# A two-layer encoder trunk on one core: stores issued later, the bias masked in DRAM, and softmax sums applied after the value product

## The chip, the cores and the metric

The kernel runs on one core of a Trainium2 chip as one program. The metric is the device time of a run in microseconds, taken as the median of several runs. A separate, profiled execution of the same program gives the views that are quoted here; its clock starts at its first instruction.

## The reference

The input is x, 2048 rows of 1024 float32. Layer A is a gated MLP that mixes rows within groups of 128; layer B is a chunked attention whose K and V come once from the residual stream after layer A. The change touches layer B and the projections around it. Reduced to what matters (16 heads of 64, chunks of 64 rows, a band of 9 chunks):

```python
h = rms_norm(x, b_norm_g)
q, z = split(h @ w_qz)                      # 1024 each
bias = rel_bias[:, clip(rel, -256, 256) + 256]
...
sc = q * 64 ** -0.5 @ kc.T + bias           # kc, vc: this chunk and the 8 before it
sc = where(valid, sc, -1e30)
o = softmax(sc) @ vc
x = x + (o * silu(z)) @ w_out
out = rms_norm(x, final_norm_g)
```

## The kernel before

Every product runs on TensorE (PE) as three matmuls of split operands: high x high, low x high, high x low (`mm3`, lines L113 to L115). The high half is a rounding copy on ScalarE (ACT), the low half a subtraction on VectorE (DVE). The 2048 rows are four tiles t = 0 to 3 of 512 rows. The order in each engine's queue is written by the framework's scheduler from the order of the program and its own estimates; at run time each engine takes its queue strictly in order, and all DMAs are issued by SyncE (SP) from one such queue. A store whose data is not ready therefore keeps every later load waiting.

The stages follow one another in the profile:

- Layer A until about 1340 us. Beside it, `rel` is copied 16 times into DRAM as `reld` (128 equal rows of 768 per head).
- The V projection (`vp`), 1340 to 1550 us: four tiles by Strassen's seven products. `v_left` splits sums of x into `Shv` and `Slv`, `v_evict` builds `v` and stores it to `vhd` (L1156). Beside it `norm` and `block` prepare the next tile of x and store it to `xtd`, and `o_sums` prepares sums of the output weight and stores their halves to `ows` (L306).
- Attention of tile 0, 1550 to about 1760 us, and of tiles 1 to 3, to about 2617 us. Tiles 1 to 3 each carry the output projection of the tile before (`bo`).
- The tail, to 2709.6 us: the output projection of tile 3.

An attention tile has eight pairs p of heads, and a pair has eight steps u (two heads, four blocks of 128 rows). `take` interleaves matmuls of the next pair's projections (`project`: Q and K, `gate`: Z) with the steps. In tile 0 the weights are loaded raw (`weights`, L210), scaled in place on GpSimd (POOL, `scaled`, L184), stored to `wk` for the later tiles (L212) and split into `wh_b` on ACT (L199) and `wl_b` on DVE (L200); four raw buffers serve these loads and others. In tiles 1 to 3 the scaled weights are loaded (L208).

Step u issues `score(u + 2)`: the product Q K into PSUM `s` (one buffer); DVE adds the bias, negates and takes the row minimum (L1328); ACT takes the exponential and its row sum `sl` (L1335); DVE inverts it (L1338); POOL scales the row of probabilities with it (L1339). The bias tile of a head is loaded as a skewed view of `reld` (`load_bias`, L1297) and two corners of 64x64 are overwritten on POOL (L1301, L1302). Then `flip(u)` transposes the block on PE (L1355, PSUM `tp`, one buffer), ACT copies it rounded (L1358), DVE subtracts (L1359). `value` multiplies with V after four steps (L1379); two adds join the halves (L1388, L1389); after the second head the gate multiplies 0.5 Z (L1396) and `og` is stored to `ogd` (L1401). For the last two pairs of tile 3 `last_og` takes the place of that store. Finished rows are normalized in `finish` (y loaded from `x2d` at L1519, scaled at L1522, stored to `out` at L1526).

## Time and profile before

| | us |
|---|---|
| median of 3 runs | 2712.83 (2712.39 to 2716.46) |
| the profiled execution | 2711.34 |
| its span, first to last instruction | 2709.6 |
| PE busy in the span | 2624.9 |
| mean granted clock of TensorE | 0.988 |

Times in the views are from the start of the span. Engines are PE, PEld (its weight load, which overlaps), DVE, ACT, POOL and SP; SPq is SP's own queue. In a row of the timeline the brackets hold the idle time of the engine before the instruction and what ended it. In a group's row, after the count, stand the busy time, the mean in ns, and the idle time before with its releasers. In the waits, after the colon, stand the total in us, the number of times and the longest. In the DMA rows stand the count, the size of one and the median time from issue to landing. The last figure but two of a row of stretches is the granted clock, then the DMA share and GB/s.

### The profile page before, as it was taken

The numbers are of one execution on the slowest core, as the hardware profiler recorded it, in microseconds if no ns is written. First come the engines' busy times: TensorE is split into PE (matmuls) and PEld (weight loads), VectorE is DVE, ScalarE is ACT, GpSimd is POOL, SyncE is SP. The second block draws the span as 40 slices with busy tenths as digits, with TensorE's granted clock in tenths as the row PEclk, the third lists the DMA queues.
The fourth block names the chain that finished last, engine by engine and source line by source line (L and its number), as shares of the span: only waits on it lengthen the run. The fifth ranks groups of instructions, "written<-read, shape, count | busy, mean of one in ns | idle before, by whom it ended". The sixth has DMA issues, their size and how long they took to land. (4 is left out here: it accounts for less than half of the span.)

```text
span 2709.6 us, 38048 instructions
## 1 busy us (share of the span) xinstructions
PE 2624.9 (97%) x12960; PEld 2194.7 (81%) x12960; DVE 1882.2 (69%) x2937; ACT 1295.4 (48%) x2296; POOL 890.3 (33%) x874
## 2 busy tenths in 40 slices
PE   8999999999999999999989989999999999999997
PEld 7788888888888888888867777788888888788875
DVE  5655676676677668667677867676678667866676
ACT  5422243433524435333355466556556555655553
POOL 3512335143351414114044344323233224223243
PEclk9999999999999999999999999999999999999999
DMA  8898999989988879768677788776688667766577
GB/s 300 310 333 328 347 363 326 329 310 351 326 310 287 304 261 324 284 214 288 238 250 259 253 270 280 254 229 200 224 265 271 200 216 241 254 199 203 180 233 244
DMA packets 274769, 735.51 MB, mean 271 GB/s; under 512 B 29584, under 2 KB 61328, under 8 KB 274576
## 3 DMA queue, kind: packets, MB, share of 16 engines
q1 hardware_dynamic: 274576, 733.09, 78.0%
q8 instruction: 103, 1.69, 0.2%
q14 instruction: 90, 0.74, 0.1%
HBM read 540.56 MB, written 181.93 MB: 267 GB/s over the span
## 5 line engine op out<-in xcount | busy, mean ns | idle before, releaser
L113 PE MATMUL P<-T,S 128*128 128x512 f32 x1248 | 495.0, 397 | 2.1 <-ACT S L376 2.1
L115 PE MATMUL P<-T,S 128*128 128x512 f32 x1248 | 489.4, 392 | 0.0
L114 PE MATMUL P<-T,S 128*128 128x512 f32 x1248 | 488.2, 391 | 0.6 <-DVE T L379 0.6
L1339 POOL TENSOR_SCALAR pr<-pr,sl 128x640 f32<-128x640 f32 (+4 forms) x256 | 198.4, 775 | 576.8 <-DVE sl L1338 498.8
L113 PE MATMUL pj<-hh_b,wh_b 128*128 128x512 f32 x768 | 321.4, 418 | 3.2 <-ACT wh_b L199 2.4
L115 PE MATMUL pj<-hh_b,wl_b 128*128 128x512 f32 x768 | 306.2, 399 | 0.1
L114 PE MATMUL pj<-hl_b,wh_b 128*128 128x512 f32 x768 | 305.2, 397 | 0.0
L1335 ACT ACTIVATE pr<-pr,nm 128x640 f32<-128x640 f32 (+4 forms) x256 | 195.4, 763 | 179.2 <-DVE nm L1328 174.3
L115 PEld LDWEIGHTS P<-T,S 128*128 128x128 f32 x1248 | 234.8, 188 | 50.3
L113 PEld LDWEIGHTS P<-T,S 128*128 128x128 f32 x1248 | 235.2, 188 | 46.7 <-ACT S L376 2.3
L114 PEld LDWEIGHTS P<-T,S 128*128 128x128 f32 x1248 | 235.1, 188 | 46.5 <-DVE T L379 1.0
L1359 DVE TENSOR_TENSOR pt<-tp,pt 128x640 fp32r<-128x640 f32 (+4 forms) x256 | 188.9, 738 | 63.4 <-ACT pt L1358 60.0
L1328 DVE CUSTOM_DVE_ANT_0 pr<-s,bias 128x640 f32<-128x640 f32 (+4 forms) x256 | 188.1, 735 | 31.9 <-PE s L1320 26.1
L1358 ACT CAST pt<-tp 128x640 fp32r<-128x640 f32 (+4 forms) x256 | 159.1, 621 | 64.7 <-PE tp L1355 60.9
L1355 PE MATMUL tp<-ident,pr 128*128 128x128 f32 x1120 | 167.1, 275 | 19.8 <-DVE pt L1359 12.5
L1355 PEld LDWEIGHTS tp<-ident,pr 128*128 128x128 f32 x1120 | 131.2, 141 | 53.3 <-issue 17.7
L115 PEld LDWEIGHTS pj<-hh_b,wl_b 128*128 128x128 f32 x768 | 146.2, 190 | 32.9 <-DVE wl_b L200 0.5
L1379 PEld LDWEIGHTS pv<-pt,V 128*128 128x128 f32 x896 | 145.2, 191 | 24.6 <-ACT pt L1358 6.1
L113 PEld LDWEIGHTS pj<-hh_b,wh_b 128*128 128x128 f32 x768 | 146.8, 191 | 21.7 <-ACT wh_b L199 3.5
L1379 PE MATMUL pv<-pt,V 128*128 128x256 f32 (+3 forms) x896 | 156.1, 323 | 5.6 <-ACT pt L1358 3.7
L114 PEld LDWEIGHTS pj<-hl_b,wh_b 128*128 128x128 f32 x768 | 146.9, 191 | 17.3
L200 DVE TENSOR_TENSOR wl_b<-raw_b,wh_b 128x1024 fp32r<-128x1024 f32 x96 | 126.8, 1320 | 33.9 <-ACT wh_b L199 32.8
(284 smaller groups left out, 5719.2 us busy)
## 6 DMA issues: line engine op xcount, KB each, us to landing
S<-hsd SPq DMA_DIRECT2D x288, 512.0 KB, 5.1
rw<-in_w_a SPq DMA_DIRECT2D x108, 512.0 KB, 6.3
A<-ytd SPq DMA_DIRECT2D x72, 512.0 KB, 5.8
raw_b<-wk SPq DMA_DIRECT2D x72, 512.0 KB, 4.0
hsd<-S SPq DMA_DIRECT2D x56, 512.0 KB, 4.2
V<-vhd SPq DMA_DIRECT2D x56, 512.0 KB, 5.3
wh_bo<-ows SPq DMA_DIRECT2D x50, 512.0 KB, 4.0
wl_bo<-ows SPq DMA_DIRECT2D x50, 512.0 KB, 5.5
```

Of the source, the lines that this page charges most:

```text
L113: first = mm(ps, lh, rh, start=first, stop=False)
L114: mm(ps, lh, rl, start=False, stop=False)
L115: mm(ps, ll, rh, start=False, stop=last)
L200: tv(wl[:], raw[:], wh[:].bitcast(F32), op=sub)
L1328: nc.vector.tensor_tensor_reduce(out=pr[:, c0:].rearrange("p (a b) -> p a b", a=nseg), in0=ps[:, :nseg, :w], in1=bias[:, c0:].rearrange("p ...
L1335: nc.scalar.activation(pr[:, c0:], pr[:, c0:], AF.Exp, scale=-1.0, bias=nm[:], accum_out=sl[:])
L1339: nc.gpsimd.tensor_scalar(pr[:, c0:], pr[:, c0:], sl[:], 1.0, op0=ALU.mult, op1=ALU.mult)
L1355: tpose(tp[:, b, :], pr[:, b * P : (b + 1) * P], ident[:])
L1358: nc.scalar.copy(oh, tp[:, b0:5, :].rearrange("p a b -> p (a b)"))
L1359: nc.vector.tensor_tensor(pt[:, 2560 + o + b0 * P : 2560 + o + 640], tp[:, b0:5, :].rearrange("p a b -> p (a b)"), oh.bitcast(F32), op=ALU ...
L1379: mm(po[:, q0 * P : q1 * P], vtl[t, p][:, i, hs], rhs, start=(i == blocks[0] and j == 0), stop=(i == 7 and j == 1),)
```

## The change

- **Bias.** The host now lays out the skewed bias, 128 x 640 per head. During layer A it is copied to `biasd[h]`, and two DMAs of 64x64 write the mask into each copy from a small table `negd`. A tile's bias is one plain load of 320 KB; the 128 memsets are gone, and the load is issued one step later (qb 2 instead of 1).
- **Probabilities.** They stay unnormalized. The row sums of a pair's eight steps go to the eight columns of one tile `sums`, inverted together at u = 7 (32 reciprocals of 128x8 in place of 256 of 128x1). `flip` at u = 6 (5 for the last pair) transposes the sums as well, ACT copies the 8x128 result to `rc`, one DMA stores it to `rcd`, and two DMAs read it back, broadcast over 64 partitions each, as `w` (128x512). The sums are complete by then, because `score` runs two steps ahead of `flip`.
- **Gate.** `gated` runs at u = 1 of the next pair: POOL multiplies w by Z, DVE multiplies 0.5 og32 by that.
- **Held stores.** `hold(n, ...)` puts a store in a list, `tick()` counts projection steps, and after n of them the store is issued with an ordering dependency (no wait at run time) on the last matmul written. Held are the stores to `xtd` (tiles above 0), `wk`, `ows`, `owf`, `vhd`, `khd`, `ogd`, `x2d`, `out` (tiles below the last), the copies of Q between partitions, and the trip of the sums. `release_all()` issues what is left before a load of y and at the ends of stages.

Counted in the compiled programs, PE gets 32 more instructions, ACT 32 more, SP 129 more DMAs; DVE 224 fewer and POOL 351 fewer.

```diff
-    reld = [dram.tile([P * 768], F32, name=f"reld{h}") for h in range(NH)]
+    rcd = [dram.tile([NPAIR, 8 * P], F32, name=f"rcd{t}") for t in range(NT)]
+    biasd = [dram.tile([P, 640], F32, name=f"biasd{h}") for h in range(NH)]
+    negd = dram.tile([P, 64], F32, name="negd")
...
-    mm, tpose = nc.tensor.matmul, nc.tensor.transpose
+    tpose = nc.tensor.transpose
+    pe = [None]
+    def mm(*args, **kw):
+        ins = nc.tensor.matmul(*args, **kw)
+        pe[0] = ins.ins.name
+        return ins
...
+    held = []
+    def tick():
+        for x_ in held:
+            x_[0] -= 1
+        for x_ in [x_ for x_ in held if x_[0] <= 0]:
+            release(x_)
+    def release(x_):
+        held.remove(x_)
+        for args in x_[1]:
+            ins = nc.sync.dma_start(*args)
+            tc.add_manual_dep(
+                ins.ins, pe[0],
+                mybir.DependencyInfo(mybir.DependencyClass.NoSync, mybir.DependencyReason.DATA),
+                reason="order",
+            )
+    def hold(n, *todo):
+        held.append([n, todo])
+    def release_all():
+        while held:
+            release(held[0])
...
             nc.scalar.copy(x3[:, ks, :], half[h][:])
-        nc.sync.dma_start(xtd[t][b][:], xt[:])
+        if t:
+            hold(4, (xtd[t][b][:], xt[:]))
+        else:
+            nc.sync.dma_start(xtd[t][b][:], xt[:])
...
             paced_by_pj(scaled(raw, (bg if c else kg)[:, :, :]))
-            nc.sync.dma_start(wk3[p][c][:], raw[:])
+            hold(1, (wk3[p][c][:], raw[:]))
         hi = split_in(raw, *w)
...
             if ph == 5:
-                nc.sync.dma_start(owf[q][:, cs], src)
+                hold(3, (owf[q][:, cs], src))
             hi, lo = (s_place(f"so{u}_{ph}{x_}") for x_ in "hl")
...
             for n, y_ in enumerate((hi, lo)):
-                nc.sync.dma_start(ows[ph, q][:, n, cs], y_[:].bitcast(F32))
+                hold(3, (ows[ph, q][:, n, cs], y_[:].bitcast(F32)))
...
+        def mask():
+            ng = acc_tile("ng")
+            nc.gpsimd.memset(ng[:, 0:64], NEG)
+            nc.sync.dma_start(negd[:], ng[:, 0:64])
+        at(start[3, 1] + 2, mask)
         at(start[1, 6] + 8, uz_open)
...
                 start[3 + h // 6, 1] + 3 + 9 * (h % 6),
-                lambda h=h: nc.sync.dma_start(
-                    reld[h].rearrange("(p c) -> p c", c=768), rel[h, :].partition_broadcast(P)
-                ),
+                lambda h=h: nc.sync.dma_start(biasd[h][:], rel[h]),
+            )
+            at(
+                start[3 + h // 6, 1] + 8 + 9 * (h % 6),
+                lambda h=h: [
+                    nc.sync.dma_start(biasd[h][0:64, 576:640], negd[0:64, :]),
+                    nc.sync.dma_start(biasd[h][64:128, 0:64], negd[64:128, :]),
+                ],
             )
...
                     )
-                nc.sync.dma_start(
-                    vhd[t][:, 4 * c : 4 * c + 4, 2 * jp + r, :], v[:].bitcast(F32)
-                )
+                hold(3, (vhd[t][:, 4 * c : 4 * c + 4, 2 * jp + r, :], v[:].bitcast(F32)))
...
             ):
+                tick()
                 if t + 1 < NT and i in (1, 4, 7, 10):
...
                     todo.pop(0)()
+        release_all()
         pt4x.close()
...
                 )
-                for x_ in (qh, ql):
-                    nc.sync.dma_start(x_[r2, :].bitcast(F32), x_[r, :].bitcast(F32))
+                hold(2, *((x_[r2, :].bitcast(F32), x_[r, :].bitcast(F32)) for x_ in (qh, ql)))
                 qt[t, p, hd] = (qh, ql)
...
                 if t + 1 < NT:
-                    nc.sync.dma_start(khd[t][p][hd], kx[:, T:].bitcast(F32))
+                    hold(4, (khd[t][p][hd], kx[:, T:].bitcast(F32)))
                 if t > 0:
...
         prs = {}
+        sums = {}
         pts = {}
...
                 bias[:],
-                reld[h][127 : 127 + P * 767].rearrange("(p c) -> p c", c=767)[:, :640],
+                biasd[h][:],
             )
-            nc.gpsimd.memset(bias[0:64, 576:640], NEG)
-            nc.gpsimd.memset(bias[64:128, 0:64], NEG)
             bias_t[t, h] = bias
...
             h = 2 * p + hd
-            if qb == 1 and (h + 1 < NH or t + 1 < NT):
+            if qb == 2 and (h + 1 < NH or t + 1 < NT):
                 load_bias(t + (h + 1) // NH, (h + 1) % NH)
...
             nm = sm.tile([P, 1], F32, tag="nm", name=f"nm{t}_{h}_{qb}", bufs=4)
-            sl = sm.tile([P, 1], F32, tag="sl", name=f"sl{t}_{h}_{qb}", bufs=4)
+            if u == 0:
+                sums[t, p] = sm.tile([P, 8], F32, tag="sl", name=f"sl{t}_{p}", bufs=2)
             nc.vector.tensor_tensor_reduce(
...
             nc.scalar.activation(
-                pr[:, c0:], pr[:, c0:], AF.Exp, scale=-1.0, bias=nm[:], accum_out=sl[:]
+                pr[:, c0:], pr[:, c0:], AF.Exp, scale=-1.0, bias=nm[:],
+                accum_out=sums[t, p][:, u : u + 1],
             )
-            nc.vector.reciprocal(sl[:], sl[:])
-            nc.gpsimd.tensor_scalar(
-                pr[:, c0:], pr[:, c0:], sl[:], 1.0, op0=ALU.mult, op1=ALU.mult
-            )
+            if u == 7:
+                nc.vector.reciprocal(sums[t, p][:], sums[t, p][:])
             prs[t, h, qb] = pr
...
                 tpose(tp[:, b, :], pr[:, b * P : (b + 1) * P], ident[:])
+            if u == sums_at(t, p):
+                tpose(tp[0:8, 5, :], sums[t, p][:], ident[:])
             o = qb * 640
...
             )
+            if u == sums_at(t, p):
+                inverse(t, p, tp[0:8, 5, :])
+        def sums_at(t, p):
+            return 5 if t + 1 == NT and p + 1 == NPAIR else 6
+        def inverse(t, p, src):
+            rc = sm.tile([8, P], F32, tag="rc", name=f"rc{t}_{p}", bufs=1)
+            nc.scalar.copy(rc[:], src)
+            w = zt[t, p, 1] = sb.tile([P, T], F32, tag="og", name=f"w{t}_{p}", bufs=2)
+            trip = [(rcd[t][p].rearrange("(a b) -> a b", b=P), rc[:])] + [
+                (
+                    w[hd * 64 : hd * 64 + 64, :],
+                    rcd[t][p, hd * T : hd * T + T].partition_broadcast(64),
+                )
+                for hd in range(2)
+            ]
+            if t + 1 == NT and p + 1 == NPAIR:
+                for args in trip:
+                    nc.sync.dma_start(*args)
+            else:
+                hold(1, trip[0])
+                hold(6, *trip[1:])
...
             nc.vector.tensor_tensor(og32[r, :], po[r, :], ot[r, :], op=ALU.add)
-            if hd == 0:
-                return
-            if hd == 1 and t + 1 == NT and p >= 6:
-                last_og(p, og32, zt[t, p])
-            elif hd == 1:
-                og = sb.tile([P, T], F32, tag="og", name=f"og{t}_{p}", bufs=2)
+        def gated(t, p):
+            og32, og = og32s[t, p], zt[t, p, 1]
+            tg(og[:], og[:], zt[t, p][:], op=ALU.mult)
+            if t + 1 == NT and p >= 6:
+                last_og(p, og32, og)
+            else:
                 nc.vector.scalar_tensor_tensor(
-                    og[:], og32[:], 0.5, zt[t, p][:], op0=ALU.mult, op1=ALU.mult
+                    og[:], og32[:], 0.5, og[:], op0=ALU.mult, op1=ALU.mult
                 )
                 o4 = og[:].rearrange("p (j r s) -> p r j s", j=2, r=2)
-                for r_ in range(2):
-                    nc.sync.dma_start(ogd[t][:, r_, p], o4[:, r_])
+                hold(3, *((ogd[t][:, r_, p], o4[:, r_]) for r_ in range(2)))
...
                 if not last:
-                    nc.sync.dma_start(x2d[t][b][:, c * 512 : c * 512 + 512], y)
+                    hold(2, (x2d[t][b][:, c * 512 : c * 512 + 512], y))
                 if (r, c) in ((1, 0), (0, 1)):
...
                 else:
+                    release_all()
                     y = sb.tile([P, 2, 512], F32, tag="bx", name=f"y{t}_{b}", bufs=1)
...
                     r0 = t * T + b * P
-                    nc.sync.dma_start(out[r0 : r0 + P, cs], y[:, c, :])
+                    if last:
+                        nc.sync.dma_start(out[r0 : r0 + P, cs], y[:, c, :])
+                    else:
+                        hold(2, (out[r0 : r0 + P, cs], y[:, c, :]))
...
                     return
+                tick()
...
             for _ in gen:
-                pass
+                tick()
...
                     done = max(done, upto)
+                    if u == 1 and before:
+                        gated(*before)
                     if u == 4:
...
         value(*before, 1)
+        gated(*before)
         run(gen)
...
         run(outs[NT - 1])
+        release_all()
...
     lo = 639 - 256
-    relr = relr[:, np.clip(np.arange(768) - lo, 0, relr.shape[1] - 1)]
+    cols = np.arange(640)[None, :] - np.arange(P)[:, None] + 127
+    relr = relr[:, np.clip(cols - lo, 0, relr.shape[1] - 1)]
     arrays = {
```

## The prediction

> **What bounds the kernel now.** I read the page's busy times first, then a table of stretches, then the waits, and last the timeline at the places where PE stood still.
>
> ```profile
> PE 2624.9 (97%) x12960; PEld 2194.7 (81%) x12960; DVE 1882.2 (69%) x2937; ACT 1295.4 (48%) x2296; POOL 890.3 (33%) x874
> ```
>
> PE is busy for 97% of the span. A change that leaves PE's matmuls alone can only win idle time and time at a low granted clock, so I look for both by stage. The columns are the stretch, its length, the busy time of PE, PEld, DVE, ACT and POOL, the granted clock, the DMA share and GB/s:
>
> ```profile
> 100.00:1340.00 1240.00, 1236.72 (x5809) 1028.77 (x5808) 840.03 (x1058) 461.64 (x731) 366.94 (x251) 1.00 0.86 310
> 1340.00:1550.00 210.00, 187.67 (x840) 151.75 (x839) 155.12 (x224) 110.93 (x218) 84.74 (x63) 0.96 0.71 246
> 1550.00:1600.00 50.00, 44.70 (x217) 35.83 (x216) 32.64 (x71) 27.80 (x59) 22.30 (x28) 1.00 0.87 277
> 1600.00:1650.00 50.00, 45.18 (x213) 36.54 (x212) 33.28 (x80) 29.00 (x63) 20.83 (x29) 0.93 0.80 267
> 1650.00:1700.00 50.00, 46.10 (x226) 37.39 (x225) 38.41 (x91) 31.57 (x74) 24.35 (x33) 0.94 0.87 289
> 1700.00:1760.00 60.00, 55.80 (x274) 44.10 (x272) 39.90 (x93) 35.97 (x75) 20.85 (x30) 0.98 0.75 248
> 1760.00:2617.00 857.00, 847.43 (x4627) 729.77 (x4627) 619.52 (x1139) 504.71 (x912) 258.00 (x346) 0.99 0.69 223
> 2617.00:2709.60 92.60, 70.36 (x321) 54.91 (x319) 64.56 (x105) 39.55 (x77) 40.83 (x38) 0.93 0.74 253
> ```
>
> Layer A has 3.3 us of idle PE in 1240 us: what the change puts there (mask and bias copies) lies under it. The idle time is in the V projection (22.3 us), attention tile 0 (5.3 + 4.8 + 3.9 + 4.2 = 18.2 us), tiles 1 to 3 (9.6 us in 857) and the tail (22.2 us). The clock takes more: 7% and 6% of 50 us in tile 0, 6.5 us, and 7% of 92.6 us in the tail, 6.5 us.
>
> What holds PE in tile 0 (start, duration, engine, line, what ended the idle time before):
>
> ```profile
> 1558.33 0.14 POOL L1301 MEMSET bias<- 64x64 f32 x1 [21.24 <-DMA bias<-reld]
> 1560.68 1.05 ACT L199 CAST wh_b<-raw_b 128x1024 fp32r<-128x1024 f32 x1 [3.43 <-POOL raw_b L184]
> 1564.70 0.39 PE L1320 MATMUL s<-K,Qh 128*128 128x256 f32 x1 [2.21 <-DVE nm L1328]
> 1593.74 1.96 DVE L200 TENSOR_TENSOR wl_b<-raw_b,wh_b 128x1024 fp32r<-128x1024 f32 x1 [0.20 <-ACT wh_b L199]
> 1596.90 0.41 PE L1355 MATMUL tp<-ident,pr 128*128 128x128 f32 x2 [2.08 <-POOL wo L315]
> 1640.95 1.90 POOL L184 TENSOR_TENSOR raw_b<-raw_b,bg 128x1024 f32<-128x1024 f32 x1 [0.60 <-DMA raw_b<-in_w_kqz]
> 1643.97 1.23 DVE L200 TENSOR_TENSOR wl_b<-raw_b,wh_b 128x1024 fp32r<-128x1024 f32 x1 [2.75 <-ACT wh_b L199]
> 1645.87 0.74 PE L1355 MATMUL tp<-ident,pr 128*128 128x128 f32 x4 [1.99 <-POOL pr L1339]
> 1692.64 1.90 POOL L184 TENSOR_TENSOR raw_b<-raw_b,bg 128x1024 f32<-128x1024 f32 x1 [3.50 <-DVE sl L1338]
> 1695.67 0.80 PE L113 MATMUL pj<-hh_b,wh_b 128*128 128x512 f32 x1 [1.65 <-ACT wh_b L199]
> ```
>
> POOL runs in order. At 1558 a mask memset that waits for its bias holds up the weight scaling (raw_b) behind it, and so ACT's wh_b and everything after; at 1596 and 1645 the transposes wait for a probability scale queued behind other POOL work; at 1692 raw_b stood behind a scale that waited for its sum. Four times PE pays: 2.21 + 2.08 + 1.99 + 1.65 = 7.9 us.
>
> **The change part by part.**
>
> *PE.* 32 transposes (128x8 to 8x128) are added. In the chain of the tail five transposes take 0.78 us, and the group's mean is 275 ns:
>
> ```profile
> 2633.66 0.80 POOL pr L1339
> 2634.51 0.78 PE tp L1355 x5
> L1355 PE MATMUL tp<-ident,pr 128*128 128x128 f32 x1120 | 167.1, 275 | 19.8 <-DVE pt L1359 12.5 <-POOL pr L1339 4.4 <-POOL wo L315 2.1
> ```
>
> So one more costs (0.78 - 0.275) / 4 = 0.126 us, 32 cost **+4.0 us**, all of it on the bounding engine; above, 32 x 0.275 = 8.8. The 32 small ACT copies run while DVE reads the same PSUM tile; without that cover they would hold the next transposes, each by about the 0.187 us of ACT's smallest row, 6 us in all:
>
> ```profile
> L1335 ACT ACTIVATION_READ_ACCUMULATOR pr<-pr,nm 128x1 f32 x256 | 48.0, 187 | 0.0
> ```
>
> *POOL and DVE.* 256 scales, 128 memsets and 224 of 256 reciprocals go. 32 multiplications w*Z come; their nearest row is A<-A,A.
>
> ```profile
> L1339 POOL TENSOR_SCALAR pr<-pr,sl 128x640 f32<-128x640 f32 (+4 forms) x256 | 198.4, 775 | 576.8 <-DVE sl L1338 498.8 <-PE s L1320 19.8 <-PE pj L115 17.1
> L1338 DVE RECIPROCAL sl<-sl 128x1 f32<-128x1 f32 x256 | 41.1, 161 | 79.8 <-ACT pr L1335 77.3
> L1301 POOL MEMSET bias<- 64x64 f32 x64 | 9.3, 145 | 105.1 <-DMA bias<-reld 105.1
> L1420 POOL TENSOR_TENSOR A<-A,A 128x512 f32<-128x512 f32 x18 | 26.4, 1483 | 11.6 <-DVE sl L1338 9.1 <-DMA A<-ogd 2.5
> ```
>
> POOL loses 198.4 + 2 x 9.3 and gains 32 x 1.48 = 47 us; DVE loses 224 x 0.161 = 36 us. Neither bounds, so this counts only through waits. Tile 0's four waits (7.9 us) and the low clock after them (6.5 us) could all go: a gain of 0 to 14.4. All four pass through an instruction that no longer exists (a memset or a scale); some of the wait may reappear at the next operand, so I take **-12 us**.
>
> The wl_b of 1593.74 took 1.96 us while POOL combined `wo`, the one of 1643.97 took 1.23. [...]
>
> *Held stores in tile 0.* The scaled weight's store to `wk` now goes out one projection step later, and its buffer (four in all) comes free only when it has landed. That is a cost, and the new order of SP's queue shows where: four raw_b loads now stand 27, 17, 10 and 9 matmuls ahead of their first matmul; in the order of before the tightest had 21.
>
> ```profile
> raw_b<-in_w_kqz SPq DMA_DIRECT2D x24, 512.0 KB, 4.7
> wk<-raw_b SPq DMA_DIRECT2D x24, 512.0 KB, 3.9
> ```
>
> A load needs 4.7 + 1.90 (raw_b) + 1.05 (wh_b) = 7.65 us. At 44.70 / 217 = 0.206 us a matmul the four have 5.6, 3.5, 2.1 and 1.9 us and lack 2.1, 4.2, 5.6 and 5.8: 17.7 us if SP issues where the order puts them, and nothing if SP, freed of waits, runs ahead. The tightest one of before (the 1640.95 row) had 4.3 us by the order, yet POOL waited 0.60 us for it: SP ran ahead there by about 3 us. With as much here 0 + 1.2 + 2.6 + 2.8 = 6.6 are left; I take **+6 us**, between 0 and 18.
>
> *V projection.*
>
> ```profile
> SPq L1156 <- DVE v L1152: 75.5, 30, 6.2
> ACT Shv L285 <- DMA ows<-so_1h: 7.3, 2, 4.3
> ACT Shv L285 <- DMA ows<-so_7h: 2.8, 1, 2.8
> ```
>
> SP stands 75.5 us at stores of `v` that are not computed yet, with loads of x behind them; held for three steps they no longer block. Against that, three S tiles waited 10.1 us for the buffers of weight halves still being stored, and those stores are held too. The first tile's order is unchanged. I take **-4 us**, between -10 (those waits gone) and +10 (doubled).
>
> *The sums' trip through DRAM, tiles 1 to 3.* A pair now issues one store of 4 KB and two broadcast loads of 128 KB: 96 DMAs, and with the masks 129 more on SP. They need about 0.43 us each, 55 us, on a queue that is no bound. One issue and the nearest landings:
>
> ```profile
> 1564.71 0.43 SPq L1297 DMA_DIRECT2D bias<-reld  x1
> ...
> ogd<-og SPq DMA_DIRECT2D x60, 128.0 KB, 3.2
> Qh<-Qh SPq DMA_DIRECT2D x64, 128.0 KB, 3.1
> SPq L208 <- DVE sl L1338: 113.5, 41, 9.3
> ```
>
> The trip takes 3.2 + 3.1 = 6.3 us of two landings. The loads stand some 2 to 2.7 us ahead of POOL's w*Z, so POOL may come about 1 us late, and behind POOL waits DVE's gate operation, behind that the next score's reduction. PE has its score tile two steps ahead, which hides a microsecond. In return DVE is 36 us freer, SP no longer stands at L208 for a reciprocal, and exp to transpose is one POOL hop shorter. Only 9.6 us of idle PE lie here; **-2 us**, between -9 and +12. Uncovered it would cost 1 us in each of 24 pairs.
>
> [...]
>
> *Tail.* The POOL hop goes (before 2634.51 the transposes stood behind A_hl combinations and the scale), and stores of the tiles before the last no longer stand among its loads.
>
> ```profile
> 2634.51 0.77 PE L1355 MATMUL tp<-ident,pr 128*128 128x128 f32 x5 [2.42 <-POOL pr L1339]
> 2676.24 0.73 PE L113 MATMUL bo<-wh_bo,Sho 128*128 128x512 f32 x2 [1.69 <-DMA wh_bo<-ows]
> ```
>
> These are 4.1 us, and the low clock is 6.5. Rows and weights come in a new order, which can put a load behind an output: **-6 us**, between -10 and +5.
>
> **Sum.** +4 - 12 + 6 - 4 - 2 - 6 = -14 us against the profiled execution's 2711.34 us: 2697. The median of the runs is 1.5 us above that execution, so I predict **2699 us**.
>
> **The rivals.** *Full relief*: SP runs ahead everywhere, every POOL wait in tile 0 goes (-14.4), the V projection gains 8, tiles 1 to 3 6 and the tail 10: +4 - 14.4 - 8 - 6 - 10 = -34, 2678 us. For it: the four waits have one engine in common. Against it: the order's tight loads.
>
> *Late weights* (the other side): the four raw_b loads go out where the order puts them, because SP is held by Q and khd copies that follow PE. PE then waits 17.7 us, the clock falls as in the two 50 us stretches of tile 0 (two more times 3.5 us), and the relief at POOL is worth only the two transposes' waits and one clock stretch, 7.6 us: +4 - 7.6 + 17.7 + 7 - 4 - 2 - 6 = +9, 2722 us. It decides from three of the four loads on.
>
> *Nothing left*: the same late weights without the clock: +4 - 12 + 17.7 - 4 - 2 - 6 = -2, 2711 us; the gain in tile 0 is eaten there.
>
> *The trip shows*: w lands late in each pair and the score tile doesn't cover it, 24 us more than the forecast, 2723 us. Against it: steps of 847 / 24 / 8 = 4.4 us give PE other work.
>
> **How the numbers follow.** Forecast 0.45 (its own range 2688 to 2707), full relief 0.13, late weights 0.20, nothing left 0.15, the trip 0.07. About 0.2%, 5.4 us, is what a measurement of this kernel can tell from no change. Faster is 0.45 + 0.13 = 0.58, same 0.15, slower 0.27. The range reaches from beyond full relief to beyond late weights, 2674 to 2728.
>
> **What would show it.** Right: tile 0's stretches with PE above 47 of 50 us and no wait of ACT wh_b on POOL behind a memset; tiles 1 to 3 at the same idle time; PE's transposes released by ACT's exp. Wrong: waits of POOL raw_b on DMA raw_b longer than 2 us and a clock below 0.95 in tile 0 (late weights); DVE waiting on POOL at the gate operation in every pair (the trip); more idle PE in the V projection behind stores of weight halves.

## The result, and the profile after

The changed kernel takes 2730.45 us (median of 4 runs, 2726.66 to 2732.58) against 2712.61 us before (4 runs, 2708.18 to 2716.46): 1.0054 of before, 95% interval 1.0037 to 1.0071, about 15 us slower. On the chips of the experiments it was measured again: 1.0056, 1.0038 to 1.0073. The forecast was 14 us faster, and the median lies 2.45 us above its range.

The page of the profiled execution (2726.66 us, span 2724.9) shows that the work went away as planned. POOL had 890.3 us before, DVE 1882.2 and PE 2624.9:

```profile
PE 2634.8 (97%) x12992; PEld 2197.8 (81%) x12992; DVE 1875.2 (69%) x2713; ACT 1301.7 (48%) x2328; POOL 717.5 (26%) x523
```

POOL gave up 173 us, and the kernel still got slower. The stages say where. Here the table of stretches begins at 1340 us and is cut at the same events in both kernels: the first score of tile 0, the first of tile 1, the last score of tile 3, and the end (columns as in the prediction). First the kernel before, then the changed one:

```profile
1340.00:1559.20 219.20, 196.87 (x881) 159.34 (x879) 158.56 (x228) 113.64 (x222) 85.48 (x66) 0.96 0.72 248
1559.20:1779.00 219.80, 200.78 (x965) 161.59 (x964) 156.29 (x357) 132.51 (x287) 96.00 (x126) 0.95 0.80 264
1779.00:2640.10 861.10, 847.48 (x4650) 729.23 (x4648) 621.59 (x1144) 505.70 (x914) 267.37 (x356) 1.00 0.69 224
2640.10:2709.60 69.50, 52.11 (x219) 40.12 (x217) 46.99 (x71) 27.68 (x52) 23.06 (x21) 0.91 0.72 246
```

```profile
1340.00:1566.80 226.80, 202.47 (x891) 163.31 (x889) 161.61 (x230) 117.17 (x226) 90.21 (x65) 0.95 0.68 239
1566.80:1790.50 223.70, 203.59 (x973) 161.23 (x973) 151.75 (x299) 131.57 (x291) 62.76 (x36) 0.96 0.81 271
1790.50:2654.40 863.90, 850.14 (x4675) 731.16 (x4673) 603.74 (x977) 510.37 (x939) 123.17 (x94) 1.00 0.71 231
2654.40:2724.90 70.50, 51.56 (x218) 38.70 (x216) 48.71 (x71) 27.19 (x52) 23.80 (x20) 0.94 0.69 243
```

Every stretch grew: the first by 7.6 us, tile 0 by 3.9, tiles 1 to 3 by 2.8, the tail by 1.0. Of the 7.6 us, 2.4 lie in layer A: the first matmul of the V projection starts at 1353.43 us instead of 1351.07, and from there to the first score it is 213.3 us against 208.1, 5.2 more. (That first matmul starts between 1349.3 and 1354.5 us in the profiles of all the kernels below, whatever their edits, so the 2.4 are not laid to a cause.) The mean granted clock is the same, 0.988; by stages it differs by 0.01, in the tail by 0.03.

Two reserves hold for all that follows. Stretches of one kernel differ by 1 to 3 us between executions: a second profile of the changed kernel has 225.1 and 865.2 us for the second and third. And the only profile of the kernel before is of the first result, 2711.34 us; on the chips of the experiments that kernel takes 2717 to 2718 us, so a stretch of an experiment can look longer against it than its edit makes it, by some of these 6 us. Sizes that rest on less are called open.

What PE, its weight load and ACT wait for in the changed kernel (the total in us, the number of times, the longest):

```profile
PE tp L1401 <- DVE pt L1407: 18.6, 18, 2.8
PE tp L1401 <- ACT rc L1420: 4.3, 6, 1.8
PEld tp L1401 <- ACT rc L1420: 9.4, 13, 2.2
ACT rc L1420 <- DVE pt L1407: 8.5, 11, 1.2
```

The transposes' waits for POOL's scale (4.4 us) and wo (2.1) are gone, but their wait for DVE rose from 12.5 us to 18.6, and a new releaser stands beside it: `rc`, ACT's copy of the transposed sums, which the prediction had costed at nothing. The timeline of one such flip, in tile 1:

```profile
1823.31 0.71 PE L1401 MATMUL tp<-ident,pr 128*128 128x128 f32 x5
1823.85 0.27 PE L1403 MATMUL tp<-ident,sl 128*8 128x128 f32 x1
1824.16 0.69 ACT L1406 CAST pt<-tp 128x640 fp32r<-128x640 f32 x1 [1.88 <-PE tp L1403]
1824.89 0.82 DVE L1407 TENSOR_TENSOR pt<-tp,pt 128x640 fp32r<-128x640 f32 x1 [0.51 <-ACT pt L1406]
1825.48 0.19 ACT L1382 ACTIVATION_READ_ACCUMULATOR pr<-pr,nm 128x1 f32 x1
1825.75 0.25 ACT L1420 COPY rc<-tp 8x128 f32<-8x128 f32 x1
```

ACT's rc starts 0.04 us after DVE has finished with the tile, not beside it, and so do 22 of the 32 copies; none starts sooner. It waits for DVE, and the next flip, which needs the only `tp` buffer, waits for it. In all ACT stands 8.5 us for DVE there, 11 times. Why the two do not run side by side is not shown: no run gives the sums a PSUM tile of their own.

SP has a new wait as well. It stands at the sums' stores until rc is there, with weight loads behind them, and then at the loads of w until the store has landed:

```profile
SPq L145 <- ACT rc L1420: 70.0, 29, 4.8
SPq L145 <- DMA rcd<-rc: 21.6, 14, 3.0
```

In tile 0, POOL stands 67.6 us (6 times) until w has landed. Where w comes late, the next weight stands behind it, as it once did behind a memset. Tile 0 of the changed kernel:

```profile
1631.14 1.29 POOL L1466 TENSOR_TENSOR w<-w,Z 128x512 f32<-128x512 f32 x1 [20.50 <-DMA w<-rcd]
1632.39 1.90 POOL L220 TENSOR_TENSOR raw_b<-raw_b,bg 128x1024 f32<-128x1024 f32 x1
1632.47 2.37 DVE L1470 SCALAR_TENSOR_TENSOR w<-og,w 128x512 f32<-128x512 f32 x1 [1.59 <-POOL w L1466]
1634.76 0.28 DVE L1375 CUSTOM_DVE_ANT_0 pr<-s,bias 128x128 f32<-128x128 f32 x1
1635.10 0.39 PE L116 MATMUL s<-K,Qh 128*128 128x256 f32 x1 [1.06 <-DVE nm L1375]
```

POOL's product waits for w, the weight raw_b stands behind it, and the gate operation on DVE, released by the product, starts 0.08 us after raw_b and takes 2.37 us. Behind it stands a score's reduction, and PE waits for that. So this chain ends in the score, not in a weight. PE's waits in tile 0 show the same: those for POOL that the prediction listed are gone, and those for DVE have come. First the kernel before, then the changed one:

```profile
PE s L1320 <- DVE nm L1328: 2.9, 2, 2.2
PE tp L1355 <- DVE pt L1359: 1.4, 5, 0.4
```

```profile
PE s L116 <- DVE nm L1375: 7.0, 9, 1.7
PE tp L1401 <- DVE pt L1407: 6.4, 8, 2.7
```

### The profile page after: what moved, and what is told of

Its sections match the earlier page's. It is cut to its first block, busy times and chain, and to the rows that moved or that the text cites. A ratio compares the mean times of both kernels' runs of the same rounds, so it can differ in the third digit from the quotient of the medians.

```text
span 2724.9 us, 37287 instructions
## 1 busy us (share of the span) xinstructions
PE 2634.8 (97%) x12992; PEld 2197.8 (81%) x12992; DVE 1875.2 (69%) x2713; ACT 1301.7 (48%) x2328; POOL 717.5 (26%) x523
## 5 line engine op out<-in xcount | busy, mean ns | idle before, releaser
L116 PE MATMUL P<-T,S 128*128 128x512 f32 x3744 | 891.5, 394 | 3.1 <-ACT S L412 2.1
L116 PEld LDWEIGHTS P<-T,S 128*128 128x128 f32 x3744 | 693.8, 188 | 143.7 <-ACT S L412 2.3
L1401 PE MATMUL tp<-ident,pr 128*128 128x128 f32 x1120 | 169.6, 277 | 23.4 <-DVE pt L1407 18.6
L1406 ACT CAST pt<-tp 128x640 fp32r<-128x640 f32 (+4 forms) x256 | 159.0, 621 | 60.9 <-PE tp L1401 49.0
L1401 PEld LDWEIGHTS tp<-ident,pr 128*128 128x128 f32 x1120 | 131.6, 141 | 60.9 <-DVE pt L1407 29.9
L116 PE MATMUL Po<-To,So 128*128 128x512 f32 x768 | 176.6, 390 | 0.0
L116 PEld LDWEIGHTS Po<-To,So 128*128 128x128 f32 x768 | 143.6, 188 | 29.6
L1466 POOL TENSOR_TENSOR w<-w,Z 128x512 f32<-128x512 f32 x32 | 42.7, 1334 | 394.6 <-DMA w<-rcd 393.6
L545 DVE TENSOR_TENSOR x<-P,x 128x512 f32<-128x512 f32 x144 | 97.6, 682 | 37.9 <-PE P L116 37.6
L116 PE MATMUL Po<-To_hh,So 128*128 128x512 f32 x384 | 118.8, 389 | 1.4 <-DVE So L415 1.4
```

The costliest lines, as they stand in the source:

```text
L116: ins = nc.tensor.matmul(*args, **kw)
L545: last["evict"] = nc.vector.tensor_tensor(*args, **kw).ins.name
L1401: tpose(tp[:, b, :], pr[:, b * P : (b + 1) * P], ident[:])
L1406: nc.scalar.copy(oh, tp[:, b0:5, :].rearrange("p a b -> p (a b)"))
L1466: tg(og[:], og[:], zt[t, p][:], op=ALU.mult)
```

## The experiments

Two theories were set up first. Theory H: the held stores cost the time (they stand in front of loads, and buffers come free later). Theory U: the way of the sums costs it. The parts of the change were built alone and in pairs, then the suspected waits were taken out one at a time. All ratios are to the kernel before, run on the same chip; "us" is the ratio less one, times 2717. Three of the kernels leave out a part of the computation to price it: after_no_norm, after_rc_only and after_no_prod.

| kernel | ratio | 95% interval | us |
|---|---|---|---|
| bias_only | 1.0006 | 0.9994 to 1.0018 | +2 |
| hold_only | 1.0029 | 1.0019 to 1.0039 | +8 |
| unnorm_only | 1.0077 | 1.0056 to 1.0098 | +21 |
| bias_unnorm | 1.0117 | 1.0097 to 1.0137 | +32 |
| after_no_unnorm | 1.0012 | 1.0000 to 1.0024 | +3 |
| after_again (the change) | 1.0056 | 1.0038 to 1.0073 | +15 |
| after_no_norm | 0.9987 | 0.9977 to 0.9998 | -4 |
| after_rc_only | 0.9997 | 0.9987 to 1.0007 | -1 |
| after_rc_first | 1.0015 | 1.0006 to 1.0024 | +4 |
| after_no_prod | 1.0028 | 1.0017 to 1.0039 | +8 |
| after_v_now | 1.0065 | 1.0044 to 1.0086 | +18 |
| best2 | 1.0027 | 1.0016 to 1.0038 | +7 |
| after_act_store | 1.0041 | 1.0026 to 1.0057 | +11 |
| best3 | 1.0025 | 1.0015 to 1.0035 | +7 |
| best4 | 1.0035 | 1.0022 to 1.0048 | +10 |
| hold_wk_now | 1.0037 | 1.0022 to 1.0053 | +10 |
| best5 | 1.0035 | 1.0020 to 1.0049 | +10 |
| best6 | 1.0005 | 0.9992 to 1.0018 | +1 |

### The three parts alone and in pairs

The edits are the parts of the diff in the section on the change: bias_only is the kernel before with the hunks of `biasd` and `negd`; hold_only with `hold`, `tick` and `release_all`; unnorm_only with `sums`, `inverse` and `gated` (its own three DMAs keep their delays); bias_unnorm is the changed kernel with every other store issued at once; after_no_unnorm is the changed kernel with reciprocal and scale as before.

> The kernel before with only the bias part of the change (skewed and masked in DRAM, no memsets on POOL, load one step later). Theory H (the held stores are what costs): the bias part gains, 3 to 8 us below before, since POOL's memsets no longer hold up the weight scaling of tile 0. Theory U (the sums' way costs: the added transposes, the rc copy that the next transposes wait for, and w*Z on POOL ahead of the weights): the same here, 3 to 8 us below before. If it is slower than before, both theories lack a part.

> The kernel before with only the held stores (bias and normalization as before). Theory H: 8 to 15 us slower than before, about 5 of it in the V projection, where the loads of x for tile 0 stand behind held stores of v, the rest in tile 0. Theory U: within 5 us of before.

> The kernel before with only the unnormalized probabilities (the trip of the sums keeps its own delays; all other stores go out at once, the bias as before). Theory H: within 5 us of before, the 4 us of added transposes paid back by POOL. Theory U: 8 to 15 us slower than before, with PE's transposes waiting for rc about 4 us and POOL's w*Z waiting for its load ahead of a raw_b in tile 0.

> The changed kernel without its held stores (the trip of the sums keeps its delays). Theory H: 12 to 18 us faster than the changed kernel, so within 5 us of before. Theory U: within 5 us of the changed kernel, 10 us or more slower than before.

> The changed kernel with the probabilities normalized as before (256 reciprocals and POOL scales back, no trip); masked bias and held stores stay. If the parts add up, the sum of bias alone and holds alone: 8 us above before, so 10 us faster than the changed kernel. If the bias part helps the held stores in tile 0: at before.

Measured: +2, +8, +21, +32 and +3 us. Theory U holds for the larger share, theory H for the smaller, and neither had bias_unnorm above the change itself. The sum of the first three (31) is twice the whole change (15): the parts do not add up. Holding the stores costs 8 us alone, and takes 17 off (32 less 15) where the sums' way is there. The bias part gains nothing alone, although the memsets behind which the weight of 1558 waited are gone; this missed the 3 to 8 us that both theories expected. In its profile tile 0 is 217.0 us against 219.8, but the rest is longer. In unnorm_only and bias_unnorm PE's wait for rc is twice that of the changed kernel, tile 0 takes 236.4 and 233.5 us, and the tail 80 instead of 70. In bias_unnorm:

```profile
PE tp L1399 <- ACT rc L1418: 9.7, 10, 2.0
```

### Which step of the sums' way

```diff
 after_no_norm: no reciprocal, no transposes, no rc, no DMAs, no product
 after_rc_only: no DMAs and no product
-            tg(og[:], og[:], zt[t, p][:], op=ALU.mult)
-                    og[:], og32[:], 0.5, og[:], op0=ALU.mult, op1=ALU.mult
+                    og[:], og32[:], 0.5, zt[t, p][:], op0=ALU.mult, op1=ALU.mult
 after_no_prod: only this
-            tg(og[:], og[:], zt[t, p][:], op=ALU.mult)
 after_rc_first, in flip
+            if u == sums_at(t, p):
+                inverse(t, p, tp[0:8, 5, :])
             nc.scalar.copy(oh, tp[:, b0:5, :].rearrange("p a b -> p (a b)"))
...
-            if u == sums_at(t, p):
-                inverse(t, p, tp[0:8, 5, :])
```

> The changed kernel with no normalization at all: the sums are never inverted, transposed or applied, and the gate multiplies by Z alone (32 reciprocals, 32 transposes, 32 rc copies, 96 DMAs and 32 POOL products left out). Theory trip (the way of the sums costs the time, not the rest): at least 15 us faster than the changed kernel, so at or below before. Theory order (the held stores and the new order of SP's queue cost it): 5 to 8 us faster only, the price of the transposes, so still 10 us above before.

> The same, but the sums are inverted, transposed and copied to rc; only the three DMAs of a pair and the POOL product are left out (the probabilities stay unnormalized). Theory trip, with PE's part in it: 4 us of transposes and 4 us of waits for rc, so 8 us above the kernel with no normalization; what is left to the changed kernel is the DMAs and POOL. Theory order: less than 5 us above it.

> The changed kernel with ACT's rc copy ahead of its copy of the same block, so that it no longer waits for DVE's reading of that block. If the waits of PE's transposes for rc (4.3 us) and of their weight loads (9.4 us) are real costs: 3 to 6 us faster than the changed kernel. If they only take the place of the wait for DVE: within 2 us of it.

> The changed kernel unaltered, on the chip of the experiments, as their base. From its first runs: 1.0037 to 1.0071 of before, about 15 us above it. If it is below 1.0025 here, the gain read from the rc copy's place was a difference between chips.

> The changed kernel without the POOL product w*Z (the gate multiplies by w alone, Z is left out of the computation); the trip's DMAs stay and DVE waits for them itself. Theory POOL (the product stands in POOL's queue ahead of a weight and waits there for its load): tile 0 about 6 us shorter, as in the kernel without the trip's DMAs (217.6 us from the first score of tile 0 to the first of tile 1, against 223.7), and 5 to 8 us faster than the changed kernel. Theory SP (the trip's loads wait for the store to land and hold up weight loads in SP's queue): tile 0 stays at 222 us or more, within 3 us of the changed kernel.

With no normalization the kernel is 4 us faster than before and 19 faster than the changed one, so the way of the sums is what costs. Without its DMAs and product, but with rc where the change puts it, 16 of these 19 us are gone: transposes and the late rc by themselves are worth 3 us, not the 8 that one theory expected. Without the product alone 8 are gone; with rc merely copied first, 11. These three add up to 35, more than the 19, so they are not costs beside each other. The rows suggest how they hang together: a late rc delays the store, the store the loads of w, w the product and the gate, and the gate holds up DVE, on which rc waits.

The stretches of after_rc_first:

```profile
1340.00:1565.30 225.30, 201.63 (x883) 162.29 (x882) 161.97 (x230) 117.22 (x225) 88.48 (x65) 0.94 0.69 239
1565.30:1790.70 225.40, 204.16 (x973) 161.68 (x973) 152.98 (x299) 131.35 (x291) 62.93 (x36) 0.96 0.82 268
1790.70:2645.30 854.60, 845.08 (x4652) 728.16 (x4651) 600.03 (x975) 509.25 (x936) 125.21 (x94) 1.00 0.73 233
2645.30:2723.70 78.40, 59.45 (x239) 44.34 (x238) 48.42 (x73) 28.39 (x55) 23.64 (x20) 0.88 0.67 227
```

Tiles 1 to 3 take 854.6 us in place of 863.9 and 865.2, but the tail gives back 8: its matmuls rise from 218 to 239, since 15 products with V and 5 transposes that had run before the last score now run after it. Tiles 1 to 3 and tail together take 933.0 us, against 934.4 and 936.7 in the changed kernel and 930.6 before, so these stretches place only 1 to 4 us of the gain, and the rest of it is not placed. The medians moved by 8 us (2730.22 to 2722.14, on different chips), the ratios by 11, the profiled spans by 1 and 4 only (2724.9 and 2727.6 to 2723.7). The sign is clear, since the intervals of the ratios do not meet; the size is open between 1 and 11. SP's wait for rc fell from 70.0 us to 48.2.

For tile 0 the expectation of after_no_prod lay between the theories: 221.8 us (from 1564.8, the start of the first score, to 1786.6), against 217.3 without normalization and 217.6 without DMAs and product. The product in POOL's queue is a part of the cost there, not all of it.

### SP at the sums' store

```diff
 after_act_store
-                hold(1, trip[0])
+                nc.scalar.dma_start(*trip[0])
 best3: this, and rc first; best4: both, and no other store held
```

> The changed kernel with the 4 KB store of a pair's sums issued by ACT, right behind its rc copy, instead of by SP. In the changed kernel SP stands 70.0 us at these stores (29 times, up to 4.8) with weight loads behind them. Theory SP (these waits set tile 0's late weights): 5 us or more faster than the changed kernel, most of it in tile 0, where pairs 4 and 5 (first score of pair 4 to first score of pair 6) take 55 to 58 us instead of 61.5. Theory POOL (the product stands ahead of weights in POOL's queue): within 3 us of it.

> The changed kernel with rc copied first and the store of the sums on ACT. If both are costs of their own: 12 us or more faster than the changed kernel, at before or below. If they are one cost (SP waits for rc, and an earlier rc ends that wait): as with rc copied first alone, 4 us above before.

> As the last, without the held stores (masked bias and unnormalized probabilities alone). Without the two mends this pair of parts was 32 us above before. If the late rc and the store on SP made that: within 10 us of before. If the missing holds made it: 20 us above before or more.

The store on ACT takes the 70 us of SP's wait for rc out of the trace, and 4 us off the time; the intervals overlap (1.0026 to 1.0057 against 1.0038 to 1.0073), so this size is open. SP now waits at the next place, the loads of w, 59.7 us instead of 21.6:

```profile
SPq L145 <- DMA rcd<-rc: 59.7, 17, 5.7
```

With rc first as well (best3) nothing more is won: +7 against +4 of rc first alone. That is what was expected if the late rc and the store on SP are one cost. The best4 run answers what made the 32 us of bias_unnorm: with the two mends and no store held, it is 22 us faster than that, at +10 against the +7 of best3, which holds its stores. So the held stores had not gained 17 us by themselves; they had hidden a part of the rc chain. In the profiles tile 0 is 10 us shorter and tiles 1 to 3 are 10 us shorter; the tail is still 77.3 us.

### Which held stores cost

```diff
 after_v_now: vhd and xtd at once; hold_wk_now, best5: wk at once
 best6: ows and owf at once; best5 and best6 with rc first
-            hold(1, (wk3[p][c][:], raw[:]))
+            nc.sync.dma_start(wk3[p][c][:], raw[:])
...
-                hold(3, (ows[ph, q][:, n, cs], y_[:].bitcast(F32)))
+                nc.sync.dma_start(ows[ph, q][:, n, cs], y_[:].bitcast(F32))
 best2: vhd and xtd at once, rc first, and
-            tg(og[:], og[:], zt[t, p][:], op=ALU.mult)
+            (tg if t else tv)(og[:], og[:], zt[t, p][:], op=ALU.mult)
```

> The changed kernel with the stores of v and of x's tiles (vhd, xtd) issued at once. If the held stores in front of the loads of x delay tile 0's first operand: the stretch from the last V tile's first matmul to the first score is 54 to 57 us instead of 60, and 3 to 5 us faster than the changed kernel. If not: 59 us or more and within 2 us.

> The changed kernel with three mends at once: vhd and xtd stored at once, rc copied first, and in tile 0 the product w*Z on DVE instead of POOL. If the three costs are as the runs so far show (3 to 5 us in the V projection, 6 in tile 0, 4 or more at rc): at or below before, 15 us or more faster than the changed kernel. If DVE takes the wait that POOL had: 5 us above before.

> The kernel before with the held stores, except that the scaled weights (wk) are stored at once, as before. Held stores alone were 8 us above before, 5 of it in tile 0. Theory late weights (a raw buffer comes free a store later, so its next load is late): 4 us or more faster than held stores alone, within 4 us of before, and pairs 4 and 5 of tile 0 take 55 to 57 us instead of 60.9. If the other held stores ahead of the loads in SP's queue do it: within 2 us of held stores alone.

> The changed kernel with rc copied first and wk stored at once. Theory late weights: at before or below (rc first alone was 4 us above it), pairs 4 and 5 of tile 0 at 55 to 58 us instead of 62.4. If not: as rc first alone, 1.0006 to 1.0024 of before.

> The changed kernel with rc copied first and the output weight's halves (ows, owf) stored at once. In held stores alone fourteen of these stores stand in SP's queue ahead of the loads for pair 6, and PE waits up to 5.2 us for a weight there. Theory blocks of held stores: pairs 4 and 5 of tile 0 take 55 to 58 us instead of 62.4, and 4 to 6 us faster than with rc first alone, so at before, 0.998 to 1.001. If the trip's own DMAs are what is left: 61 us or more there, and within 2 us of rc first alone.

Storing v and x at once won nothing (+18), and from the last V tile's first matmul to the first score it still took 60.1 us (1503.6 to 1563.7). Neither did storing the scaled weights at once: hold_wk_now is at +10 against +8 of hold_only, best5 at +10 against +4, and pairs 4 and 5 take 64.0 and 66.3 us, not 55 to 58. But the timeline of hold_wk_now shows stores that stand in front of the weights. SP goes through the halves of the output weight one after another, each waiting for its producer, and only then issues the weight loads of the next pairs:

```profile
1681.62 0.78 SPq L143 DMA_DIRECT2D ows<-so_1h  x1
...
1705.61 0.42 SPq L143 DMA_DIRECT2D ows<-so_4l  x1
1706.09 1.34 SPq L244 DMA_DIRECT2D raw_b<-in_w_kqz  x2
...
1713.26 1.89 POOL L218 TENSOR_TENSOR raw_b<-raw_b,bg 128x1024 f32<-128x1024 f32 x1 [1.73 <-DMA raw_b<-in_w_kqz]
1716.28 0.79 PE L114 MATMUL pj<-hh_b,wh_b 128*128 128x512 f32 x1 [5.18 <-ACT wh_b L233]
```

So best6 issues those at once. It is the best of the kernels with all three parts: 1.0005 of before, 0.9992 to 1.0018, no measurable difference, 14 us faster than the changed one. Against rc first alone (+4) the intervals overlap, but the V projection shows what changed. From its first matmul to the first score it takes 208.1 us before, 209.0 to 210.7 in the four kernels that hold no stores but the trip's, 212.0 to 215.4 in the fourteen that hold them all or all but v, x or wk, and 209.4 in best6. So it is the held halves of the output weight that cost the V projection its 3 to 5 us.

The way there goes through the loads of x for tile 0 (`xr_b`). Without held stores two of the four have gone out when the last V tile is 1.3 us old; with them the first goes out 2.6 to 4.7 us after its start and the last three from 7.9 us on, behind a store of v; in best6 two have gone out before it starts. ACT stands at the rounding copy of that x (`hh_b`) until it has landed, with `Shv` of the last V tile behind it, and DVE takes the low halves (`hl_b`) ahead of the last `Slv`. When x is late, so is `Slv`, and PE waits for it. First the kernel before:

```profile
1511.96 1.44 SPq L165 DMA_DIRECT2D xr_b<-xtd  x2
1516.12 3.50 DVE L169 TENSOR_TENSOR hl_b<-xr_b,hh_b 128x1024 fp32r<-128x1024 f32 x3 [3.45 <-issue]
1516.99 1.05 ACT L168 CAST hh_b<-xr_b 128x1024 fp32r<-128x1024 f32 x1 [3.59 <-DMA xr_b<-xtd]
1524.38 0.51 PE L115 MATMUL vp<-vwh,Slv 128*128 128x512 f32 x1 [2.21 <-DVE Slv L286]
```

The changed kernel:

```profile
1515.09 1.94 SPq L201 DMA_DIRECT2D xr_b<-xtd  x3
1519.85 1.05 ACT L204 CAST hh_b<-xr_b 128x1024 fp32r<-128x1024 f32 x1 [2.58 <-DMA xr_b<-xtd]
1522.55 3.49 DVE L205 TENSOR_TENSOR hl_b<-xr_b,hh_b 128x1024 fp32r<-128x1024 f32 x3
1531.40 0.64 PE L116 MATMUL vp<-vwh,Slv 128*128 128x512 f32 x1 [4.65 <-DVE Slv L322]
```

And best6:

```profile
1524.36 0.50 PE L116 MATMUL vp<-vwh,Slv 128*128 128x512 f32 x1 [2.22 <-DVE Slv L322]
```

This wait of PE is 1.9 to 2.2 us in the kernels without held stores and in best6, and 4.0 to 5.1 in the others. From the last V tile's first matmul to the first score it is 54.2 us before (1505.0 to 1559.2), 59.7 in the changed kernel (1507.1 to 1566.8), 60.3 with rc first and 56.6 in best6 (1505.0 to 1561.6).

In tile 0 best6 wins nothing:

```profile
1561.60:1789.50 227.90, 204.23 (x973) 162.80 (x973) 151.32 (x299) 130.08 (x291) 61.19 (x36) 0.96 0.81 266
```

That is 2.5 us more than with rc first alone, so the stores seen ahead of the weights in hold_wk_now are not shown to make tile 0 long. The half of best6's expectation on tile 0 missed with it: pairs 4 and 5 of tile 0 (first score of pair 4 to first of pair 6) still take 61.7 us (1674.3 to 1736.0), as in the changed kernel (1674.8 to 1736.3), against 55.2 before (1668.9 to 1724.1). They take 54.1 without normalization and 56.9 without the trip's DMAs and product, 59.1 with the store on ACT, and 63.6 without the product. So with the stores held it is the trip's DMAs that lengthen these pairs, and by which queue position was not settled. In hold_only, with no trip at all but POOL's scales as before, the same pairs take 60.9: held stores and scales together give about the same, by a way that stays open.

The product on DVE in tile 0 (best2) won nothing that shows beside rc first: +7 against +4, where at or below before was expected.

## Why the prediction was wrong

**The steps that failed.** "The 32 small ACT copies run while DVE reads the same PSUM tile": this cover did not exist. The copy starts when DVE has finished, and it stands in the ring of the single `tp` buffer; the section on the result shows the rows. The text gave the price if the cover were gone as 6 us, 0.187 for each copy. The copies last 0.25 us, 8 us in all. As a direct wait that price was high enough: PE stands 4.3 us behind rc (its weight load, which overlaps, 9.4), and transposes and late rc without the trip cost 3 us. What the prediction did not see is what hangs on rc: the store, for which SP stands 70.0 us, and behind it w, POOL and the gate. With the copy moved ahead of DVE's reading the kernel is 8 us faster by the medians and 11 by the ratios, of the 15 it had lost.

The second step is one that the sum lacks: the trip had a term in tiles 1 to 3 but none in tile 0, where POOL has the weights to scale as well. Tile 0 takes 223.7 us with the trip and 217.6 without its DMAs and product, 6 us less, and POOL stands 67.6 us there for w. From the issue of the store to POOL's product it is 6.9 us (median of 32, up to 16.4 in tile 0); the rows had given 6.3.

**The POOL relief (-12 us).** This term was too large, by how much is open between two comparisons. With the masks in DRAM and nothing normalized, tile 0 takes 217.3 us. That is 2.5 us less than before, but this kernel holds stores as well; hold_only, which has the held stores and POOL's old work, takes 224.8, 7.5 us more. First after_no_norm, then hold_only:

```profile
1566.00:1783.30 217.30, 201.72 (x966) 161.76 (x966) 146.90 (x292) 129.75 (x284) 55.15 (x29) 0.95 0.82 270
```

```profile
1565.00:1789.80 224.80, 202.71 (x966) 160.51 (x966) 155.95 (x357) 133.49 (x287) 94.68 (x126) 0.96 0.81 261
```

The part of the term that stood for the clock did not come: 0.95 before, 0.95 without normalization, 0.96 in the changed kernel (bias_only alone has 0.98). Of the four waits of 7.9 us two are for POOL by name and two for what stood behind a POOL operation. They are gone, but PE now waits for DVE at other places of tile 0, 13.4 us for the score's reduction and for pt where it was 4.3 (8.2 without normalization). A wait's length is not what its removal gains: that is its distance to the next operand that is late.

**The transposes (+4.0 us).** Each takes 0.27 us in the timeline and ends 0.10 us after the five others, which take 0.71 together; the term had 0.126. Kernels with and without transposes and rc differ by 3 us (after_no_norm to after_rc_only, intervals overlapping): not contradicted.

**Held stores in tile 0 (+6 us).** Sign and size are near the forecast (hold_only: tile 0 takes 1789.8 - 1565.0 = 224.8 us against 219.8, though from another chip), but the mechanism is not shown. The late store of the scaled weight to wk is not it: stored at once, tile 0 takes 227.8 us in hold_wk_now and 226.4 in best5. Stores held for three steps do arrive at SP in blocks ahead of weight loads, but with the halves of the output weight stored at once tile 0 is no shorter. The cause of these 5 us stays open; that the number came near is luck.

**V projection (-4 us).** It went to +5.2. The step that failed is "held for three steps they no longer block": SP waits 83.3 us for v now instead of 75.5, and the loads of x go out later than before, behind the held stores. Holding these stores did not end the wait in SP's queue, it moved it. The prediction had the halves of the output weight as its danger, and their held stores are what cost, though by the loads of x and not by the S buffers.

**The trip in tiles 1 to 3 (-2 us).** They lost 2.8. With rc first they take 854.6 us instead of 861.1, but with the tail it is 933.0 against 930.6 before, so no gain is shown. POOL was to come about 1 us late for w; it waits 393.6 us for it over the whole run, 25 times, though most of that costs nothing, since POOL has little else to do there.

**Tail (-6 us).** 70.5 us against 69.5: nothing was won. The wait for POOL's scale (2.4 us) is gone, and one of 1.8 us for rc came.

Of the rivals two came nearest in time, late weights (2722) and the trip (2723). The trip was seen, in tile 0 and not as a wait of 1 us in each of 24 pairs: the gate waits for POOL 8 times, 9.0 us in all. Of late weights the trace has POOL waiting for raw_b up to 5.7 us in tile 0, but the clock there stays at 0.96, and the store that was to make them late is not the cause. Both were priced with everything else as forecast; the loss came with less relief and with a loss in V beside them.

## What to carry to other kernels

Where an edit is costed at nothing because another engine's work hides it, look first in a trace whether the two run side by side on one tile, and ask what waits behind the edit if they do not; here none of 32 copies started before DVE was done, and one copy moved ahead took back 11 of the 15 us by the ratios. A store that is held back in an ordered queue need not wait less (here 83.3 us against 75.5) and is in the way of what now stands behind it, so count what it is moved in front of, and test such holds one kind of store at a time. When several parts are changed together, build them alone and in pairs: here +2, +8 and +21 made +15, and a part that looked like a gain of 17 us was covering another part's cost. And cut stages at events, not at times, and look at what moved across the cut, before a shorter stage is called a gain.

## What the runs showed of the hardware

The gate operation on DVE takes 0.69 us by itself and 2.37 us where POOL's raw_b starts just before it. Two places in tile 0 of the changed kernel, without and with:

```profile
1659.88 0.69 DVE L1470 SCALAR_TENSOR_TENSOR w<-og,w 128x512 f32<-128x512 f32 x1
...
1692.59 1.90 POOL L220 TENSOR_TENSOR raw_b<-raw_b,bg 128x1024 f32<-128x1024 f32 x1
1692.67 2.37 DVE L1470 SCALAR_TENSOR_TENSOR w<-og,w 128x512 f32<-128x512 f32 x1 [0.23 <-POOL w L1466]
```

The slow one ends 0.55 us after raw_b does (1695.04 against 1694.49 us), and so does the one at 1632.47 (1634.84 against 1634.29); why it lasts until then is not shown. The change lines the two up: the product releases DVE's gate, and POOL starts the next weight, if it is there, right behind the product. So in tile 0 four of seven gates of the changed kernel take 1.84 to 2.37 us, before one of seven took 2.12.
